# A two-layer hybrid decoder trunk: two mLSTM operands turned on TensorE instead of VectorE, and the loads and orders of the first two chunks rearranged

## The chip, the cores and the metric

The kernel runs on one core of one Trainium2 chip. The metric is the device time of one launch in microseconds (us), from the first to the last instruction of the program. Below, PE is TensorE's matmuls, PEld its weight loads, DVE is VectorE, ACT is ScalarE, POOL is GpSimd and SP is the sync engine, whose queue issues nearly all transfers.

## The reference

Two layers run over 256 tokens of 1024 features, all in float32. Each layer is a half-weighted SwiGLU, a mixer of three parallel branches, another half-weighted SwiGLU and a gated embedding:

```python
for l in range(DEPTH):
    x = x + 0.5 * swiglu(rms_norm(x, norm_ffn1[l]), ffn1_w_gu[l], ffn1_w_down[l])
    x = x + hybrid_mixer(rms_norm(x, norm_mix[l]), w_in[l], ...)
    x = x + 0.5 * swiglu(rms_norm(x, norm_ffn2[l]), ffn2_w_gu[l], ffn2_w_down[l])
    gate = jax.nn.sigmoid(rms_norm(x, norm_ple[l]) @ ple_w_gate[l])
    x = x + gate * (p[l] @ ple_w_proj[l])
return rms_norm(x, final_norm)
```

The mixer multiplies the normed tokens by one wide matrix `w_in` and splits the columns: a short gated convolution, an mLSTM with four heads (queries and keys of 128, values of 256), an indexed sparse attention that keeps the 64 best keys of each query, and three sigmoid gates that merge the branches.

## The kernel before

**Weights.** Each float32 weight tile that a transfer brings (`raw`, five buffers) is split in two: `wh` is a copy in the matmul type that ScalarE makes (L157), `wl` is the remainder that VectorE makes (L158). Each has four buffers of 4 x 512 columns. Every product is then three matmuls, L203, L204 and L205 in `mm3` (or six at L391 in the down projection). A `raw` buffer is free for the next transfer only when VectorE has made its `wl`.

**Stages.** In a feed-forward, `gate_up(c)` makes chunk c of 256 hidden columns for both token blocks, and `down_mm` adds the chunk before it into four accumulators. The first chunk of the first layer has loads of its own: four `raw` tiles (`first_gu`), split in eight pieces (`first_split`), with the tokens' transposes between them. In the mixer, `project` runs one block of 512 columns of `w_in` at a time: 4608, 5120, then the mLSTM queries (1536) and keys (2048), its values (2560, 3072), then 512, 1024, 0, 3584 and on.

**Side work.** What isn't a projection (the sparse attention `dsa`, the mLSTM gates and heads, the turns) are generators in two queues. `tick()` takes one step of the head of each queue, and `project` calls it four times, once for each half of the weights and each token block. A step's instructions are so traced between the matmuls of a projection. The order on each engine is then laid out by the tile planner, from this order as priority and from when it believes each operand to be ready; it may put a later instruction in front of an earlier one that it thinks is not ready. Every engine runs its own list strictly in order.

**The turn of queries and keys.** A projection leaves tokens on the partitions; the heads need features there. `qk_T` (L627) copies through `turn` (L277): 16 VectorE transposes at L281, each of 32 partitions, in four steps. `turn` is also used for the attention queries, the convolution and the feed-forwards. Elsewhere four TensorE transposes into one PSUM tile `tp` (two buffers) are followed by a copy on ScalarE, as at L551 and L553.

**The start.** ScalarE's queue loads the first 256 columns of x; SP loads the weights of chunk 0 and the rest of x. After them `load_gains` (L132) issues seven small transfers of gains and biases on SP, and turns the gains with one TensorE transpose (L117) and a copy. Only then do the loads of chunk 1 follow on SP. The final instruction of `first_split` on ScalarE is kept in `last`; `tc.issue_after(i)` puts all that is traced inside it, on the engine of `i`, behind `i`.

Of the kernel before, what the change touches and what calls it, by code (L numbers as in the profile page):

```python
# [10 lines left out]
F32 = mybir.dt.float32  # L11
F32R = mybir.dt.float32r
AF = mybir.ActivationFunctionType
# [3 lines left out]
P = 128  # L17
T = 256
NB = 2
# [18 lines left out]
def trunk_kernel(  # L38
# [7 lines left out]
    nc = tc.nc  # L46

    cpool = ctx.enter_context(tc.tile_pool(name="cpool", bufs=1))
# [9 lines left out]
    def nm(s):  # L58
        uid[0] += 1
        return f"{s}_{uid[0]}"  # L60
# [4 lines left out]
    def tps(shape=(P, 4, P)):  # L65
        return psum.tile(list(shape), F32, name=nm("tp"), tag="tp", bufs=2)
# [21 lines left out]
    x = []  # L88
# [3 lines left out]

    def load_x(q, c0, c1):
        for b in range(NB):
            last = q.dma_start(x[b][:, c0:c1], x_in[0, b * P:(b + 1) * P, c0:c1]).ins
        return last

    load_x(nc.scalar, 0, 256)

# [2 lines left out]
    mhalf = cpool.tile([P, 8], F32, name="mhalf")  # L102
    mh0 = cpool.tile([P, 8], F32, name="mh0")
    nc.vector.memset(mh0, -0.5)
    nc.scalar.activation(mhalf, mh0, AF.Copy)
    first_rows = cpool.tile([16, P], F32, name="first_rows")
    nc.sync.dma_start(first_rows, norm_ffn1.rearrange("l (k p) -> (l k) p", p=P))
    ident = cpool.tile([P, P], F32, name="ident")
    make_identity(nc, ident)
    gain_rows = cpool.tile([88, P], F32, name="gain_rows")  # L110
# [3 lines left out]
    def turn_gains(rows, c0):  # L114
        n = rows.shape[0]
        gps = tps((P, n))
        nc.tensor.transpose(gps, rows, ident[:n, :n])  # L117
        return nc.vector.tensor_copy(gains[:, c0:c0 + n], gps).ins
# [13 lines left out]
    def load_gains():  # L132
        r0 = 0
        for src in (norm_mix, norm_ffn2, norm_ple, mlstm_norm):
            nc.sync.dma_start(gain_rows[r0:r0 + 16, :], src.rearrange("l (k p) -> (l k) p", p=P))
            r0 += 16
        nc.sync.dma_start(gain_rows[r0:r0 + 24, :], conv_w.rearrange("l j (k p) -> (l j k) p", p=P))
        nc.sync.dma_start(bif[:, 0, :], mlstm_b_i.rearrange("l h -> h l"))
        nc.sync.dma_start(bif[:, 1, :], mlstm_b_f.rearrange("l h -> h l"))
        turn_gains(gain_rows, 16)  # L140

    zrow = cpool.tile([HM, T], F32, name="zrow")
    nc.vector.memset(zrow, 0.0)
# [8 lines left out]
    def split_tiles(shape):  # L152
        return (wpool.tile([P] + shape, F32R, name=nm("wh"), tag="wh"),
                wpool.tile([P] + shape, F32R, name=nm("wl"), tag="wl"))
# [23 lines left out]
    def gu_tiles(hi, lo):  # L178
        return [(hi[:, j].rearrange("p g n -> p (g n)"), lo[:, j].rearrange("p g n -> p (g n)"))
                for j in range(4)]  # L180

    def load_gu(src, k0, c):
# [4 lines left out]
            split(hi[:, :, g, :], lo[:, :, g, :], raws[g])  # L187
        return gu_tiles(hi, lo)

    def load_rows(src, k0):  # L190

        hi, lo = split_tiles([2, D])
        for k in range(2):
            raw = raw_tile([D])
            nc.sync.dma_start(raw, src[(k0 + k) * P:(k0 + k + 1) * P, :])
            split(hi[:, k, :], lo[:, k, :], raw)
        return [(hi[:, k, :], lo[:, k, :]) for k in range(2)]

# [78 lines left out]
    def turn(dst, src):  # L277

        for i in range(4):
            for j in range(4):  # L280
                nc.vector.transpose(  # L281
                    dst[32 * j:32 * j + 32].rearrange("p f (b i t) -> p b f i t", b=NB, i=4)[:, :, :, i, :],
                    src[32 * i:32 * i + 32].rearrange("p b (f j a) -> p b f j a", j=4, a=32)[:, :, :, j, :])
            if i < 3:
                yield

    def rms_scale(b, tag="r"):

# [30 lines left out]
    def ffn(xs, w_gu, w_down, next_norm, before_last=None, first=None):  # L319
        dn = None  # L320
        act = act_of(xs)

        def gate_up(c):
            at = mid([P, 2, 2, T], F32R)
            ps = [acc() for _ in range(NB)]
            groups = [(0, 4), (4, 4)]
            ks = {}

            def run(b, k0, n):
                for k in range(k0, k0 + n):  # L330
                    mm3(ps[b], act(b, k), ks[k], k == 0, k == KD - 1)

            s = half([P, NB, FCH])

            def finish(b):
                r = xs[b][2]
                nc.scalar.activation(s[:, b, :], ps[b][:, :FCH], AF.Silu, scale=r)  # L337
                nc.vector.scalar_tensor_tensor(s[:, b, :], ps[b][:, FCH:], r, s[:, b, :], op0=ALU.mult, op1=ALU.mult)  # L338

            def turn_pe(b):  # L340
                split_T(lambda f: s[:, b, f * P:(f + 1) * P], 2,
                        lambda f, m: at[:, 0, f:f + m, b * P:(b + 1) * P],
                        lambda f, m: at[:, 1, f:f + m, b * P:(b + 1) * P])
                return
                yield

            def turn_dve():
                st = half([P, 2, T])
                yield from turn(st, s)
                split(at[:, 0], at[:, 1], st)  # L350

            if c == 0 and first:
                ks.update(enumerate(first))
            else:
                for k0, n in groups:
                    for i, t in enumerate(load_gu(w_gu, k0, c)):
                        ks[k0 + i] = t
            if c == 0 and first:
                for k0 in range(0, KD, 2):
                    for b in range(NB):  # L360
                        run(b, k0, 2)
                for b in range(NB):
                    finish(b)
                turns = [turn_dve()]
            elif c == 0:
                for b in range(NB):
                    run(b, 0, KD)
                    tick()
                    finish(b)
                turns = [turn_dve()]  # L370
            else:
                for k0, n in groups:
                    for b in range(NB):
                        run(b, k0, n)
                        tick()
                for b in range(NB):
                    finish(b)
                turns = [turn_pe(b) for b in range(NB)] if c == NFC - 1 else [turn_dve()]
            queues[0].extend(turns)
            return at, turns  # L380

        def down_mm(act, ks, c, b):
            at, turns = act
            for t in turns:
                drain(t)
            for f in range(2):
                ah, al = (at[:, i, f, b * P:(b + 1) * P] for i in range(2))
                wh, wl = ks[f]
                for a, w in ((ah, wh), (ah, wl), (al, wh)):
                    for n in range(2):  # L390
                        nc.tensor.matmul(dn[b][n], a, w[:, n * 512:(n + 1) * 512],  # L391
                                         start=c == 0 and f == 0 and a is ah and w is wh,
                                         stop=c == NFC - 1 and f == 1 and a is al)
            tick()

        ats = {0: gate_up(0)}
        for c in range(NFC - 2):
            ats[c + 1] = gate_up(c + 1)
            if c == 0:
                dn = [[acc() for _ in range(2)] for _ in range(NB)]  # L400
            ks = load_rows(w_down, 2 * c)
            for b in range(NB):
                down_mm(ats[c], ks, c, b)
            del ats[c]
        c = NFC - 2
        ats[c + 1] = gate_up(c + 1)
        extra = before_last() if before_last else None
        k2 = [load_rows(w_down, 2 * (c + i)) for i in range(2)]
        new = []
        for b in range(NB):  # L410
            for i in range(2):
                down_mm(ats[c + i], k2[i], c + i, b)
            for n in range(2):
                xs_ = x[b][:, n * 512:(n + 1) * 512]
                nc.vector.scalar_tensor_tensor(xs_, dn[b][n], 0.5, xs_, op0=ALU.mult, op1=ALU.add)
            new.append(next_norm(b))
        return new, extra


    def mixer(l, xs, next_norm):  # L420
# [23 lines left out]
        for b in range(NB):  # L444
            q = ps1[b]
# [181 lines left out]
        def qk_T(nat):  # L627
            tt = mid([P, HM, T])
            qk.append(tt)
            yield from turn(tt, nat)  # L630
            yield

        for c0 in (1536, 2048):
            ps = proj(c0)
            nat = mid([P, NB, 512])
# [275 lines left out]
    first, ws = [], []  # L911
# [11 lines left out]
    for i in range(4):  # L923
        fetched.append(first_gu(2 * i))
        if i < 2:
            loaded = load_x(nc.sync, 256 * (i + 1), 512 * (i + 1))
    ts = [norm_tiles(b) for b in range(NB)]
    for i in range(4):
        his = [norm_part(b, G_FFN1, ts[b], 2 * i, 2)[-1] for b in range(NB)]
# [3 lines left out]
        with tc.issue_after(his[0]), tc.issue_after(gains_ready):  # L933
            last = first_split(fetched[i], 2 * (i % 2))
    with tc.issue_after(last):
        xs = [ts[b] + (rms_scale(b),) for b in range(NB)]
    with tc.issue_after(loaded):
        load_gains()
    for l in range(DEPTH):
        xs, _ = ffn(xs, ffn1_w_gu[l], ffn1_w_down[l], lambda b: norm_block(b, G_MIX + 8 * l),  # L940
                    first=first if l == 0 else None)
# [38 lines left out]
```

## Time and profile before

| | us |
|---|---|
| three runs | 1395.53, 1397.54 (median), 1398.69 |
| the profiled execution, its own time | 1398.2 |
| its span in the trace | 1396.2 |
| PE busy | 1363.6 (98%) |
| DVE busy | 1123.7 (80%) |
| ACT busy | 720.3 (52%) |

The span begins with the first recorded instruction and ends with the last; 2.0 us of the profiled time lie outside it. Matmuls overlap in the array, so their durations are longer than their spacing: back to back, a matmul of 512 columns starts every 0.23 us though it lasts 0.39 us. A busy PE in the page therefore only says that it had work; what a stall costs is read from the starts of its matmuls. In a timeline row the bracket gives the engine's idle time before the instruction and what ended it.

### The profile page before, as it was taken

The page shows a single profiled execution, that of the slowest core. Times are in us where ns is not written, and L with a number is a line of the kernel's source. Part 1 is how long each engine was busy: PE and PEld are TensorE (multiplying, and loading weights), DVE is VectorE, ACT ScalarE, POOL GpSimd, SP SyncE. Part 2 cuts the span into 40 slices and gives each one's busy share as a digit, 9 for nine tenths or more (in the row PEclk, how much of TensorE's full clock was granted, in tenths as well). Part 3 has the DMA queues.
Part 4 walks back from the last instruction along what each step waited for, and adds up shares of the span by engine and source line. Part 5 has one row for each costly group of instructions (what it writes and reads, how often), then busy time and mean ns, then how long its engine had stood idle before and what let it go on. Part 6 is the DMA issues. An engine that isn't in the chain of part 4 may idle for free.

```text
span 1396.2 us, 17264 instructions
## 1 busy us (share of the span) xinstructions
PE 1363.6 (98%) x6124; PEld 1111.8 (80%) x6124; DVE 1123.7 (80%) x2099; ACT 720.3 (52%) x1127; POOL 22.7 (2%) x42
## 2 busy tenths in 40 slices
PE   7999999799999999999999999998999999999997
PEld 6888888687788888888888888886768888888886
DVE  5978879979965688878788888799799556888876
ACT  6544465465454464444664444563655446444454
POOL 0000000000000000000000000000000000000000
PEclk9999999999999999999999999999999999999999
DMA  7766556254475546666555666554445655555661
GB/s 226 222 213 198 182 175 196 83 190 121 151 241 181 181 154 201 204 194 217 172 163 183 197 205 201 174 166 144 143 126 179 222 181 181 182 181 185 196 215 46
DMA packets 163427, 250.33 MB, mean 179 GB/s; under 512 B 7964, under 2 KB 101260, under 8 KB 163340
## 3 DMA queue, kind: packets, MB, share of 16 engines
q1 hardware_dynamic: 162700, 247.91, 55.3%
q8 instruction: 48, 0.79, 0.2%
q0 software_dynamic: 352, 1.06, 0.2%
q14 instruction: 39, 0.32, 0.1%
q10 hardware_dynamic: 288, 0.26, 0.1%
HBM read 248.14 MB, written 1.06 MB: 178 GB/s over the span
## 4 chain that ended last, share of the span: by engine, by line
PE 87%; DVE 10%; issue 1%; ACT 1%; DMA 0%; POOL 0%; SPq 0%; POOLq 0%; ACTq 0%; DVEq 0%
PE acc L205 22%; PE acc L204 22%; PE acc L203 22%; PE acc L391 17%; DVE mid L281 4%; DVE wl L158 2%; PE tp L262 2%; DVE score L504 1%; DVE m L503 1%; PE acc L675 1%; PE acc L458 1%; DMA x<-in_x_dram 0%; ACT wh L157 0%; DVE mid L722 0%; DVE big L524 0%
## 5 line engine op out<-in xcount | busy, mean ns | idle before, releaser
L158 DVE TENSOR_TENSOR wl<-raw,wh 128x1024 fp32r<-128x1024 f32 (+1 forms) x472 | 555.0, 1210 | 105.2 <-ACT wh L157 103.0
L157 ACT ACTIVATE wh<-raw 128x1024 fp32r<-128x1024 f32 (+1 forms) x472 | 473.9, 1043 | 227.4 <-issue 92.6
L204 PE MATMUL acc<-wl,xh 128*128 128x512 f32 (+1 forms) x1384 | 541.9, 392 | 13.8 <-DVE wl L158 13.8
L203 PE MATMUL acc<-wh,xh 128*128 128x512 f32 (+1 forms) x1384 | 546.4, 395 | 0.9 <-ACT wh L157 0.9
L205 PE MATMUL acc<-wh,xl 128*128 128x512 f32 (+1 forms) x1384 | 541.7, 392 | 0.0
L204 PEld LDWEIGHTS acc<-wl,xh 128*128 128x128 f32 x1384 | 262.3, 190 | 67.9 <-DVE wl L158 15.9
L203 PEld LDWEIGHTS acc<-wh,xh 128*128 128x128 f32 x1384 | 262.2, 189 | 58.1 <-issue 3.9
L205 PEld LDWEIGHTS acc<-wh,xl 128*128 128x128 f32 x1384 | 262.4, 190 | 53.8
L281 DVE STREAM_TRANSPOSE half<-half 32x128 f32<-32x128 f32 x640 | 193.6, 303 | 9.5
L391 PE MATMUL acc<-wh,mid 128*128 128x512 f32 x704 | 198.3, 391 | 0.0
L391 PEld LDWEIGHTS acc<-wh,mid 128*128 128x128 f32 x704 | 131.0, 188 | 27.4 <-ACT mid L265 0.9
L391 PE MATMUL acc<-wl,mid 128*128 128x512 f32 x352 | 108.6, 390 | 0.0
L338 DVE SCALAR_TENSOR_TENSOR half<-acc,r,half 128x256 f32<-128x256 f32 x88 | 42.1, 481 | 78.8 <-ACT half L337 78.8
L157 ACT ACTIVATE mid<-half 128x512 fp32r<-128x512 f32 x40 | 25.3, 633 | 142.9 <-DVE half L281 142.9
L337 ACT ACTIVATE half<-acc,r 128x256 f32<-128x256 f32 x88 | 41.7, 473 | 107.9 <-PE acc L205 107.8
L391 PEld LDWEIGHTS acc<-wl,mid 128*128 128x128 f32 x352 | 66.1, 188 | 13.9
L281 DVE STREAM_TRANSPOSE mid<-mid 32x256 f32<-32x256 f32 x160 | 69.7, 436 | 3.4
L272 ACT ACTIVATE xh<-tp,gains 128x128 fp32r<-128x128 f32 x128 | 41.7, 362 | 19.7 <-PE tp L262 11.3
L204 PE MATMUL acc<-wl,big 128*128 128x512 f32 x128 | 50.0, 390 | 0.0
L205 PE MATMUL acc<-wh,big 128*128 128x512 f32 x128 | 49.8, 389 | 0.0
L203 PE MATMUL acc<-wh,big 128*128 128x512 f32 x128 | 49.8, 389 | 0.0
L273 DVE SCALAR_TENSOR_TENSOR xl<-tp,gains,xh 128x128 fp32r<-128x128 f32 x128 | 40.7, 346 | 8.8 <-ACT xh L272 8.0
(180 smaller groups left out, 722.8 us busy)
## 6 DMA issues: line engine op xcount, KB each, us to landing
raw<-in_ffn_w_gu_dram SPq DMA_DIRECT2D x172, 512.0 KB, 5.1
raw<-in_w_in_dram SPq DMA_DIRECT2D x128, 512.0 KB, 4.3
raw<-in_ffn_w_down_dram SPq DMA_DIRECT2D x88, 512.0 KB, 4.6
raw<-in_mlstm_w_out_dram SPq DMA_DIRECT2D x16, 512.0 KB, 4.2
raw<-in_w_o_dram SPq DMA_DIRECT2D x16, 512.0 KB, 4.1
raw<-in_ple_w_gate_dram SPq DMA_DIRECT2D x16, 512.0 KB, 5.2
raw<-in_attn_w_out_dram SPq DMA_DIRECT2D x8, 512.0 KB, 3.6
raw<-in_conv_w_out_dram SPq DMA_DIRECT2D x8, 512.0 KB, 4.7
```

What stands on the lines that cost most here:

```text
L157: made = nc.scalar.activation(hi, v, AF.Copy).ins
L158: nc.vector.tensor_tensor(lo, v, hi.bitcast(F32), op=ALU.subtract)
L203: nc.tensor.matmul(ps, ah, wh, start=start, stop=False)
L204: nc.tensor.matmul(ps, ah, wl, start=False, stop=False)
L205: nc.tensor.matmul(ps, al, wh, start=False, stop=stop)
L262: turned[0] = nc.tensor.transpose(tp[:, j, :], src_of(k0 + j), ident).ins
L272: his.append(nc.scalar.activation(hi, tp[:, j:j + 1, :], AF.Copy, scale=g).ins)
L273: nc.vector.scalar_tensor_tensor(lo, tp[:, j:j + 1, :], g, hi.bitcast(F32), op0=ALU.mult, op1=ALU.subtract)
L281: nc.vector.transpose(dst[32 * j:32 * j + 32].rearrange("p f (b i t) -> p b f i t", b=NB, i=4)[:, :, :, i, :], src[32 * i:32 * i + 32].rea ...
L337: nc.scalar.activation(s[:, b, :], ps[b][:, :FCH], AF.Silu, scale=r)
L338: nc.vector.scalar_tensor_tensor(s[:, b, :], ps[b][:, FCH:], r, s[:, b, :], op0=ALU.mult, op1=ALU.mult)
L391: nc.tensor.matmul(dn[b][n], a, w[:, n * 512:(n + 1) * 512], start=c == 0 and f == 0 and a is ah and w is wh, stop=c == NFC - 1 and f == 1 ...
```

## The change

The queries' and keys' turn becomes four TensorE transposes and one ScalarE copy for each token block, in two steps instead of four. A first, unused Silu is put on ScalarE at the very start. The seven transfers of `load_gains` move behind the weight loads of the second down projection, and the transpose of the gains moves to chunk 5. ScalarE's instructions of chunk 1 are put behind the last split of chunk 0.

```diff
@@ at the start
+    junk0 = cpool.tile([P, 8], F32, name="junk0")
+    nc.scalar.activation(junk0, mh0, AF.Silu)
     nc.scalar.activation(mhalf, mh0, AF.Copy)
@@ def load_gains():
-        turn_gains(gain_rows, 16)
@@ def load_rows(src, k0):
-            nc.sync.dma_start(raw, src[(k0 + k) * P:(k0 + k + 1) * P, :])
+            fetched_last[0] = nc.sync.dma_start(raw, src[(k0 + k) * P:(k0 + k + 1) * P, :]).ins
@@ new
+    def pe_turn(dst, src):
+
+        for b in range(NB):
+            tp = tps()
+            for f in range(4):
+                nc.tensor.transpose(tp[:, f, :], src[:, b, f * P:(f + 1) * P], ident)
+            nc.scalar.activation(dst[:, :, b * P:(b + 1) * P], tp, AF.Copy)
+            yield
@@ def ffn
         for c in range(NFC - 2):
-            ats[c + 1] = gate_up(c + 1)
+            with ExitStack() as order:
+                if first and c == 0:
+                    order.enter_context(tc.issue_after(last))
+                ats[c + 1] = gate_up(c + 1)
+            if first and c == 5:
+                turn_gains(gain_rows, 16)
...
             ks = load_rows(w_down, 2 * c)
+            if first and c == 1:
+                with tc.issue_after(fetched_last[0]):
+                    load_gains()
@@ def qk_T(nat):
-            yield from turn(tt, nat)
-            yield
+            yield from pe_turn(tt, nat)
@@ before the layers
-    with tc.issue_after(loaded):
-        load_gains()
```

## Rows read from the trace of the kernel before

**Rows 1.** The page: busy time of each engine, and the chain's shares by engine.

```profile
PE 1363.6 (98%) x6124; PEld 1111.8 (80%) x6124; DVE 1123.7 (80%) x2099; ACT 720.3 (52%) x1127; POOL 22.7 (2%) x42
...
PE 87%; DVE 10%; issue 1%; ACT 1%; DMA 0%; POOL 0%; SPq 0%; POOLq 0%; ACTq 0%; DVEq 0%
```

**Rows 2.** Table by stretch of 5 us in the first layer's mixer, columns first.

```profile
core 0: us, PE busy (x) PEld busy (x) DVE busy (x) ACT busy (x) POOL busy (x), PEclk, DMA share, GB/s
270.00:275.00 5.00, 1.03 (x5) 0.53 (x3) 4.71 (x12) 1.63 (x2) 0.00 (x0) 0.94 0.02 8
275.00:280.00 5.00, 4.72 (x11) 3.76 (x12) 5.00 (x12) 2.94 (x7) 0.00 (x0) 0.50 0.65 197
...
340.00:345.00 5.00, 3.81 (x12) 2.96 (x13) 4.94 (x12) 3.92 (x6) 0.00 (x0) 0.76 0.17 27
```

**Rows 3.** The chain in order of time: start, us, what; one run of matmuls.

```profile
38.85 5.44 PE acc L391 x24
```

**Rows 4.** Timeline of PE, both mixers: start us, us, engine line op, tiles, shape, count.

```profile
261.85 0.39 PE L203 MATMUL acc<-wh,xh 128*128 128x512 f32 x1
265.28 0.50 PE L204 MATMUL acc<-wl,xh 128*128 128x512 f32 x1 [3.04 <-DVE wl L158]
...
275.28 0.80 PE L204 MATMUL acc<-wl,xh 128*128 128x512 f32 x1 [4.25 <-DVE wl L158]
...
280.14 1.05 PE L658 MATMUL acc<-mid,mid 128*128 128x256 f32 x2
...
949.28 0.39 PE L203 MATMUL acc<-wh,xh 128*128 128x512 f32 x1
...
967.16 0.66 PE L658 MATMUL acc<-mid,mid 128*128 128x256 f32 x2
```

**Rows 5.** Timeline of DVE in the first layer's mixer.

```profile
242.31 0.87 DVE L281 STREAM_TRANSPOSE mid<-mid 32x256 f32<-32x256 f32 x2
...
263.53 0.44 DVE L281 STREAM_TRANSPOSE mid<-mid 32x256 f32<-32x256 f32 x1
263.99 2.36 DVE L158 TENSOR_TENSOR wl<-raw,wh 128x1024 fp32r<-128x1024 f32 x2
...
308.34 0.75 DVE L710 SCALAR_TENSOR_TENSOR mid<-acc,r,mid 128x512 f32<-128x512 f32 x1 [3.23 <-PE acc L205]
```

**Rows 6.** Groups of instructions: count, busy us, mean ns of one, idle before, releaser.

```profile
L281 DVE STREAM_TRANSPOSE mid<-mid 32x256 f32<-32x256 f32 x160 | 69.7, 436 | 3.4
L553 ACT ACTIVATE half<-tp 128x512 f32<-128x512 f32 x12 | 7.0, 584 | 2.4 <-PE tp L551 2.4
```

**Rows 7.** Timeline of PE around four transposes of the sparse attention.

```profile
308.14 0.60 PE L551 MATMUL tp<-ident,big 128*128 128x128 f32 x4
...
308.81 0.40 PE L204 MATMUL acc<-wl,xh 128*128 128x512 f32 x1
```

**Rows 8.** Timeline of ACT, a weight copy that waits for its transfer.

```profile
268.78 1.06 ACT L157 ACTIVATE wh<-raw 128x1024 fp32r<-128x1024 f32 x1 [10.53 <-DMA raw<-in_w_in_dram]
```

**Rows 9.** Timeline of PE at the start.

```profile
16.51 0.39 PE L204 MATMUL acc<-wl,xh 128*128 128x512 f32 x1
20.45 0.27 PE L117 MATMUL tp<-ident,gain_rows 88*128 88x88 f32 x1 [3.55 <-issue]
...
28.13 0.50 PE L204 MATMUL acc<-wl,xh 128*128 128x512 f32 x1 [0.53 <-DVE wl L158]
```

**Rows 10.** Timeline of SP's queue at the start (issues of transfers).

```profile
8.56 0.60 SPq L135 DMA_DIRECT2D gain_rows<-in_norm_mix_dram  x1
...
13.76 2.05 SPq L173 DMA_DIRECT2D raw<-in_ffn_w_gu_dram  x4
...
41.42 9.21 SPq L173 DMA_DIRECT2D raw<-in_ffn_w_gu_dram  x4
```

**Rows 11.** Timeline of ACT at the start.

```profile
17.77 1.06 ACT L157 ACTIVATE wh<-raw 128x1024 fp32r<-128x1024 f32 x1 [3.71 <-DMA raw<-in_ffn_w_gu_dram]
18.74 0.61 ACT L272 ACTIVATE xh<-tp,gains 128x128 fp32r<-128x128 f32 x2
...
24.11 1.28 ACT L337 ACT_TABLE_LOAD   x1 [1.03 <-PE acc L205]
...
25.78 1.05 ACT L157 ACTIVATE wh<-raw 128x1024 fp32r<-128x1024 f32 x1
```

More of the change, by code (lines that the diff above doesn't have):

```diff
@@ L94, in load_x @@
         for b in range(NB):
-            last = q.dma_start(x[b][:, c0:c1], x_in[0, b * P:(b + 1) * P, c0:c1]).ins
-        return last
+            q.dma_start(x[b][:, c0:c1], x_in[0, b * P:(b + 1) * P, c0:c1])
     load_x(nc.scalar, 0, 256)
@@ L188, in load_gu @@
         return gu_tiles(hi, lo)
+    fetched_last = [None]
     def load_rows(src, k0):
@@ L925, in trunk_kernel @@
         if i < 2:
-            loaded = load_x(nc.sync, 256 * (i + 1), 512 * (i + 1))
+            load_x(nc.sync, 256 * (i + 1), 512 * (i + 1))
     ts = [norm_tiles(b) for b in range(NB)]
```

## The prediction

> **What bounds the kernel now.** I read the page's busy shares first, then its chain, then the table by stretch, and only then the timelines of the stretches that the table picked out. PE is busy 98% of the span and carries 87% of the chain [rows 1]; the reader should see that a change pays only where PE stalls, and costs wherever it adds to PE. DVE carries 10% of the chain, so some stretch hangs on it. The table shows where: between 270 and 275 us PE has 1.03 us of work while DVE is full (4.71), and in the next 5 us PE runs at a granted clock of 0.50, which is the lower of its two levels, 1.2 GHz [rows 2]. PE's timeline names the wait: it stands for 3.04 and 4.25 us, both times for `wl` of L158 [rows 4]. DVE's timeline shows why `wl` is late. From 242.31 to 263.53 it does 24 of the 32 turns of queries and keys, alternating with the top-k of the sparse attention, and only then the next two splits [rows 5]. The wait for raw weights on ACT, 10.53 us [rows 8], follows from it: a raw buffer comes free when DVE has split it. The second layer repeats this from 949.28 on [rows 4].
>
> The price of these stalls: back to back, 24 matmuls take 5.44 us [rows 3], 0.227 each. From 261.85 to 280.14 the trace starts 36 matmuls of 512 columns, worth 8.2 us; they take 18.3, so 10.1 us are lost, the stand-stills and the slow clock behind them. In the second layer, from 949.28 to 967.16, there are also 36: 17.9 less 8.2 is 9.7 [rows 3, 4]. Together 19.8 us.
>
> **The turn moved, what it removes.** A turn is 16 instructions of 436 ns [rows 6], two a layer: 32 x 0.436 = 14.0 us less on DVE in each layer. Take the same order with the turns cut out. The splits of 263.99 have 24 turns in front of them, 10.5 us, and so would start at 253.5; PE first misses them at 265.28 - 3.04 = 262.2 [rows 4, 5], so they are ready (two take 2.36) about 6 us ahead. The next splits have all 32 turns in front, and move up by 14.0 against a second stall that needs 4.25 plus what the first gave back, 7.3 in all. The raw buffers come free earlier by the same 10 to 14 us, so the transfers behind the wait on ACT do too. Both stalls go, and the slow clock with them. The order after the change isn't known, since the planner lays it out anew. If it is worse, the bound is that half of the 19.8 stays (as if only the first pair of splits moved up); it can't give more than 19.8 here. I take 19.8, because the margin is some 6 us and the turns are pure ballast in this queue.
>
> What is late next? DVE has a second full stretch in each layer, where PE waits for the softmax: between 340 and 345 it loses 1.19 us idle and, at a clock of 0.76, 0.24 x 3.81 = 0.9 more [rows 2], 2.1 us, and the like in the second layer. At 308.34 DVE had caught up and waited 3.23 us for PE [rows 5]; work saved before that point isn't carried over it. I leave this loss where it is: 0, with 4.2 as the gain if a new order heals it.
>
> **What it adds.** Each turn is two groups of four transposes, so eight groups over both layers. The group at 308.14 is followed by one matmul of 512 columns before the row at 308.81: 0.67 - 0.227 = 0.44 us on PE [rows 3, 7]. 8 x 0.44 = 3.5 us, in full on the path, as PE is the bound. ACT gets eight copies like L553, 584 ns each [rows 6], 4.7 us beside an engine that is 52% busy [rows 1]: nothing, while the weight copies run ahead. If they don't, each copy stands 0.58 in front of a split: at most 4.7. The copy waits for PE, and behind it on ACT wait the copies of weights for later matmuls; PE in turn would wait for a `tp` buffer at a third group if the first was not yet copied. From both sides: 0, if ACT is as free as its share says, and 10.5 us a layer, the longest wait of a weight copy [rows 8], if a turned group's copy is queued behind one. I take 0: with the turns off DVE that wait itself moves up and shrinks.
>
> On PE's price the trace is short: four transposes show 0.60 us from first start to last end [rows 7]. The Trainium skill (TensorE: Matmul & The Clock Gate, Part 4: PE-mode transpose) gives about 275 ns for one in a kernel's context; 32 of them unoverlapped would be an estimated 8.8 us instead of 3.5 and the sum 1382. The trace disagrees: they start closer together than that.
>
> **The start.** From 16.51 to 28.13 PE starts 19 matmuls of 512 columns, worth 4.3 us, in 11.6: 7.3 us are lost [rows 3, 9]. Three things hold it. PE stands 3.55 us in front of L117, whose rows come by the seven small transfers [rows 9]; that transpose moves to chunk 5, where the rows have long landed, and costs the same there. SP issues the seven from 8.56 on and the weights of chunk 1 only at 13.76 [rows 10]; these now go 5.2 us sooner. And ACT waits 3.71 us, to 17.77, for the first of these weights, with the last pieces of chunk 0 behind it in its list [rows 11]; the new order puts chunk 1 behind them. So the work that began at 18.74 can begin at about 14.6, when PE's last transposes are done (an estimate: ACT's idle time begins at 17.77 - 3.71 = 14.06): 4.1 us sooner. The table load of 1.28 us at 24.11 goes, because the Silu at the start fetches that table in idle time. The 1.03 us in front of it go too, as PE is early; but one weight copy, 1.06, which was done at 17.77, now comes after. 4.1 + 1.28 + 1.03 - 1.06 = 5.4 us. Ends: 3.3, if two more copies of 1.05 go in front of the one PE needs, and 7.3, all of the loss. I take 5.4.
>
> On the table load, the row shows 1.28 us and the next instruction right behind it [rows 11]. The Trainium skill (ScalarE: Activation LUTs, What ACT_TABLE_LOAD costs) counts 2.66 us with a drain; by that the sum would be 1.4 us lower. No drain shows here.
>
> The seven transfers now stand on SP between the weights of the second down projection and those of chunk 3, issued at 41.42. They took 5.2 us of SP's queue. There, four issues take 9.21 us, where four without waits took 2.05 [rows 10]: SP spends 7.2 us waiting for raw buffers, and that covers them. Price 0; if the cover is gone, 5.2 once.
>
> **Sum.** 1398.2 (profiled time) - 19.8 - 5.4 + 3.5 = 1376.5. The median of the runs is 0.7 under the profiled time; I say 1376. About 0.2%, 2.8 us, is what a measurement of this kernel can tell from no change.
>
> **The rivals.**
> - *Half of it.* The planner's new order leaves one of the two stalls in each layer: 9.9 less gain, 1386. For it: the top-k stays in front of the splits. Against: the margin of 6 us. 0.10.
> - *More.* The second full stretch heals as well (4.2) and the start gives 7.3: 1370. For it: DVE has slack; against: it waits for PE at 308.34 [rows 5]. 0.06.
> - *The gain is given back later.* PE comes some 8 us earlier to the softmax in each layer while DVE is not earlier there: 16 us back, 1392. Against: DVE loses 14 us of work, more than PE's path. 0.05.
> - *Slower.* PE's transposes wait for ScalarE. `tp` has two buffers and ACT's list is in order; a copy behind a weight copy that waits 10.53 us [rows 8] stops PE, and each restart costs slow clock, as the 2.4 us lost at 0.50 in 275 to 280 [rows 2]. Two layers: 2 x 12.9 = 26, 1402. It decides from 21.7 us in all (19.8 + 5.4 - 3.5), 10.9 a layer. For it: such a wait exists; against: it comes after 258, when the values' first projection, where the turns now sit, is over. 0.06.
> - *The clock falls around the transposes.* If a group dropped the clock, it would be low for the 9 us of the four groups and 5 more in each layer, as in 275 to 280 [rows 2]: half of 14 twice, 14 us, 1390. After the group at 308.14 the next matmuls last 0.40, those of full clock, 2.4 GHz [rows 7]. The Trainium skill (TensorE: Matmul & The Clock Gate, Part 4) says that transposes don't count as busy for the clock gate; here no row shows a fall behind one. 0.03.
>
> **How the numbers follow.** Forecast 0.70, at 1376, by its bounds 1370 to 1383. The range goes to 1369 and 1391; the slower case and the far part of the given-back one are left out. Faster by over 0.2%: 0.70 + 0.10 + 0.06 + 0.03 and 0.02 of the given-back case, 0.91; within: 0.03; slower: 0.06.
>
> **What would show it.** After the change: no `wl` wait over 1 us on PE in the mixer, granted clock 1.00 through it; 96 turns of the form on `mid` left of 160 (64 fewer over both layers), and 32 new transposes of 0.11 us spacing; ACT's new copies at 0.58 us; no L117 at the start, one Silu table load less, and PE's first steady matmul of chunk 1 near 22.7. Wrong would be: waits of PE for ACT at a `tp`, a stall that grows at the softmax, or a hole in the feed-forward near 45 us, behind the seven transfers.

## The result and the profile after

| | before | after |
|---|---|---|
| median of the runs, us | 1397.57 (1395.53 to 1398.69) | 1374.26 (1374.13 to 1376.19) |
| the profiled execution, its own time | 1398.2 | 1374.13 |
| its span | 1396.2 | 1372.3 |
| mean granted clock | 0.991 | 0.998 |

The changed kernel takes 0.9835 of the time before (95% interval 0.9819 to 0.9851), 23.3 us less. The forecast was 1376.0, from 1369 to 1391.

The code has grown, so lines have moved: the three matmuls of `mm3` are L205 to L207 (L203 to L205 before), the 32x32 turn is L283 (L281), the head's first matmul L676 (L658), the down projection L402 (L391), the softmax's transposes L570 (L551). The new transposes are L294 and their copies L295.

First the page of the changed kernel: busy time by engine, the chain's shares, and two groups (count, busy us and mean ns, idle before, releaser).

```profile
PE 1357.8 (99%) x6156; PEld 1110.4 (81%) x6156; DVE 1095.6 (80%) x2035; ACT 722.6 (53%) x1135; POOL 24.9 (2%) x42
...
PE 93%; DVE 5%; ACT 1%; issue 1%; POOL 0%; POOLq 0%; ACTq 0%
...
L206 PE MATMUL acc<-wl,xh 128*128 128x512 f32 (+1 forms) x1384 | 538.3, 389 | 0.7 <-DVE wl L158 0.7
...
L283 DVE STREAM_TRANSPOSE mid<-mid 32x256 f32<-32x256 f32 x96 | 41.8, 436 | 1.5
```

PE's share of the chain rose from 87% to 93%, DVE's fell from 10% to 5% [rows 1]. Of the 160 turns of this form [rows 6] 96 are left. PE has 32 instructions more and 5.8 us less busy time, since fewer of its matmuls ran at the lower clock (mean granted clock 0.991 before, 0.998 now). The remainders `wl` kept PE waiting 13.8 us in all, by the page of before; now it is 0.7, at the start:

```profile
L204 PE MATMUL acc<-wl,xh 128*128 128x512 f32 (+1 forms) x1384 | 541.9, 392 | 13.8 <-DVE wl L158 13.8
```

The table by stretch of 5 us, changed kernel, through the stretch that answers to [rows 2] and through the softmax behind it:

```profile
core 0: us, PE busy (x) PEld busy (x) DVE busy (x) ACT busy (x) POOL busy (x), PEclk, DMA share, GB/s
255.00:260.00 5.00, 5.00 (x23) 4.14 (x23) 4.76 (x13) 2.39 (x3) 1.16 (x1) 1.00 0.25 91
260.00:265.00 5.00, 5.00 (x23) 4.13 (x22) 3.10 (x3) 2.31 (x4) 0.00 (x0) 1.00 0.81 243
...
325.00:330.00 5.00, 3.08 (x11) 2.33 (x12) 4.89 (x13) 4.63 (x6) 0.00 (x0) 0.84 0.23 52
330.00:335.00 5.00, 5.00 (x21) 3.77 (x19) 4.84 (x11) 2.49 (x3) 0.00 (x0) 0.81 0.65 206
```

DVE is as full as before until 260 us, then it has air (3.10 of 5), and PE works through at the full clock. The stall at the softmax is still there, 14 us earlier.

VectorE's list has a new order as well. Before, no split stands between 242.31 and 263.99 [rows 5]; now two come at 242.69 and 246.05, among the rounds of the top-k. The first of them:

```profile
242.69 1.22 DVE L158 TENSOR_TENSOR wl<-raw,wh 128x1024 fp32r<-128x1024 f32 x1
```

PE's timeline of the changed kernel, both mixers. L503 is a matmul group of the indexed attention just ahead of the turns, L676 the first matmul of the mLSTM heads; of the four groups of new transposes in each layer the first is shown:

```profile
238.36 1.14 PE L503 MATMUL acc<-akT,half 64*128 64x256 f32 x8
...
242.67 0.60 PE L294 MATMUL tp<-ident,mid 128*128 128x128 f32 x4
...
266.38 0.59 PE L676 MATMUL acc<-mid,mid 128*128 128x256 f32 x2
...
917.08 1.14 PE L503 MATMUL acc<-akT,half 64*128 64x256 f32 x8
...
945.11 0.59 PE L676 MATMUL acc<-mid,mid 128*128 128x256 f32 x2
```

The same attention group in the kernel before (L484 there):

```profile
243.97 1.14 PE L484 MATMUL acc<-akT,half 64*128 64x256 f32 x8
...
931.40 1.14 PE L484 MATMUL acc<-akT,half 64*128 64x256 f32 x8
```

From that attention group to the heads PE needs 266.38 - 238.36 = 28.0 us. Before, the way from 243.97 to 280.14 [rows 4] took 36.2. In the second layer it was 967.16 - 931.40 = 35.8 and is 28.0.

The start of the changed kernel, by SP's queue, ACT and PE:

```profile
8.57 6.00 SPq L173 DMA_DIRECT2D raw<-in_ffn_w_gu_dram  x4
...
35.06 0.42 SPq L136 DMA_DIRECT2D gain_rows<-in_norm_mix_dram  x1
```

```profile
14.20 0.64 ACT L274 ACTIVATE xh<-tp,gains 128x128 fp32r<-128x128 f32 x2 [0.57 <-PE tp L264]
...
18.49 1.05 ACT L157 ACTIVATE wh<-raw 128x1024 fp32r<-128x1024 f32 x1
19.44 0.46 ACT L348 ACTIVATE half<-acc,r 128x256 f32<-128x256 f32 x1
```

```profile
19.70 0.39 PE L207 MATMUL acc<-wh,xl 128*128 128x512 f32 x1
20.90 0.73 PE L205 MATMUL acc<-wh,xh 128*128 128x512 f32 x2 [0.81 <-ACT wh L157]
22.38 0.50 PE L206 MATMUL acc<-wl,xh 128*128 128x512 f32 x1 [0.75 <-DVE wl L158]
```

The weights of chunk 1 are issued from 8.57 on, not from 13.76 [rows 10]. ACT finds them landed at 18.49 and goes on to its Silu without a table load [rows 11]. The matmul that stood at 28.13 [rows 9] starts at 22.38, 5.75 us earlier. The first matmul of the down projection goes from 38.69 to 32.95, 5.7 us earlier; below this is "the first down projection".

### The profile page after: what moved, and what is told of

The parts are those of the page before. It is cut to its first block, busy times and chain, and to the rows that moved or that the text cites. A ratio compares the mean times of both kernels' runs of the same rounds, so it can differ in the third digit from the quotient of the medians.

```text
span 1372.3 us, 17274 instructions
## 1 busy us (share of the span) xinstructions
PE 1357.8 (99%) x6156; PEld 1110.4 (81%) x6156; DVE 1095.6 (80%) x2035; ACT 722.6 (53%) x1135; POOL 24.9 (2%) x42
## 3 DMA queue, kind: packets, MB, share of 16 engines
q0 software_dynamic: 352, 1.06, 0.2%
HBM read 248.14 MB, written 1.06 MB: 182 GB/s over the span
## 4 chain that ended last, share of the span: by engine, by line
PE 93%; DVE 5%; ACT 1%; issue 1%; POOL 0%; POOLq 0%; ACTq 0%
PE acc L205 24%; PE acc L207 24%; PE acc L206 24%; PE acc L402 18%; PE tp L264 2%; DVE mid L283 2%; DVE wl L158 1%; PE acc L693 1%; PE acc L477 1%; DVE mid L740 0%; DVE big L543 0%; DVE mx L551 0%; PE acc L128 0%; PE tp L570 0%; DVE big L558 0%
## 5 line engine op out<-in xcount | busy, mean ns | idle before, releaser
L205 PE MATMUL acc<-wh,xh 128*128 128x512 f32 (+1 forms) x1384 | 544.8, 394 | 0.8 <-ACT wh L157 0.8
L207 PE MATMUL acc<-wh,xl 128*128 128x512 f32 (+1 forms) x1384 | 538.5, 389 | 0.0
L205 PEld LDWEIGHTS acc<-wh,xh 128*128 128x128 f32 x1384 | 260.6, 188 | 57.3 <-issue 3.9
L207 PEld LDWEIGHTS acc<-wh,xl 128*128 128x128 f32 x1384 | 260.3, 188 | 53.0
L283 DVE STREAM_TRANSPOSE half<-half 32x128 f32<-32x128 f32 x640 | 193.9, 303 | 9.5
L402 PE MATMUL acc<-wh,mid 128*128 128x512 f32 x704 | 198.5, 392 | 0.0
L402 PEld LDWEIGHTS acc<-wh,mid 128*128 128x128 f32 x704 | 131.0, 188 | 27.3 <-ACT mid L267 0.9
L402 PE MATMUL acc<-wl,mid 128*128 128x512 f32 x352 | 108.6, 390 | 0.0
L402 PEld LDWEIGHTS acc<-wl,mid 128*128 128x128 f32 x352 | 66.1, 188 | 13.8
L274 ACT ACTIVATE xh<-tp,gains 128x128 fp32r<-128x128 f32 x128 | 41.7, 363 | 19.8 <-PE tp L264 11.4
L207 PE MATMUL acc<-wh,big 128*128 128x512 f32 x128 | 49.9, 390 | 0.0
L205 PE MATMUL acc<-wh,big 128*128 128x512 f32 x128 | 49.8, 389 | 0.0
L283 DVE STREAM_TRANSPOSE mid<-mid 32x256 f32<-32x256 f32 x96 | 41.8, 436 | 1.5
```

What stands on the lines that cost most here:

```text
L205: nc.tensor.matmul(ps, ah, wh, start=start, stop=False)
L207: nc.tensor.matmul(ps, al, wh, start=False, stop=stop)
L274: his.append(nc.scalar.activation(hi, tp[:, j:j + 1, :], AF.Copy, scale=g).ins)
L283: nc.vector.transpose(dst[32 * j:32 * j + 32].rearrange("p f (b i t) -> p b f i t", b=NB, i=4)[:, :, :, i, :], src[32 * i:32 * i + 32].rea ...
L402: nc.tensor.matmul(dn[b][n], a, w[:, n * 512:(n + 1) * 512], start=c == 0 and f == 0 and a is ah and w is wh, stop=c == NFC - 1 and f == 1 ...
```

## The experiments

All edits are to the changed kernel unless said otherwise. The runs were made on three chips; the kernel before took 1397.8, 1397.6 and 1397.5 us beside them. Where no interval is given, one execution was taken.

### One half of the change alone

e1 puts the queries and keys back on VectorE and keeps the start.

```diff
-            yield from pe_turn(tt, nat)
+            yield from turn(tt, nat)
+            yield
```

> The changed kernel, but with the queries' and keys' turn back on VectorE (the start's changes alone). Theory (the turn's load on VectorE stalls PE; the parts add up): 5.7 us under the kernel before, 1391.8 us, with the two stalls of some 3 and 4 us per mixer back in front of a split weight, and PE's first steady matmul of chunk 1 at 22.4. Rival (the start's gain is waited for again in the mixer, because VectorE bounds it there): within 1.5 us of the kernel before, 1397, with longer stalls in the first mixer. Rival (the planner's new layout after the start made the mixer's gain): near the changed kernel, 1376, and no stalls.

Measured: 1391.22, ratio 0.9956 (0.9943 to 0.9968). Its table by stretch:

```profile
255.00:260.00 5.00, 1.97 (x10) 1.31 (x9) 4.74 (x12) 0.00 (x0) 0.00 (x0) 1.00 0.00 0
...
265.00:270.00 5.00, 0.73 (x4) 0.31 (x2) 4.74 (x12) 1.63 (x2) 0.00 (x0) 0.83 0.01 4
270.00:275.00 5.00, 5.00 (x12) 3.98 (x13) 5.00 (x11) 3.09 (x7) 0.00 (x0) 0.50 0.76 211
```

Both stand-stills are back (PE 1.97 and 0.73 of 5, DVE full), and the slow clock with them. So they belong to the turns on VectorE and not to the start. The turn is worth 1391.22 - 1374.26 = 17.0 us, and the start alone 1397.8 - 1391.2 = 6.6.

e2 is the kernel before with nothing but the queries and keys on TensorE.

```diff
@@ def qk_T (kernel before)
-            yield from turn(tt, nat)
-            yield
+            yield from pe_turn(tt, nat)
```

> The kernel before with the queries' and keys' turn on TensorE and ScalarE, nothing else. Theory: the changed kernel's time plus the start's 5.7 us, 1380.0 us; no stall of PE for a split weight between 240 and 285 us, granted clock 1.00 there, and the start as in the kernel before (the matmul of 28.13 stays). Rival (part of the mixer's gain needs the earlier start): over 1384.

Measured: 1380.98, ratio 0.9879 (0.9866 to 0.9893). PE is full in every stretch from 240 to 285 us. The turn alone takes off 1397.8 - 1381.0 = 16.8 us, and 16.8 + 6.6 is the whole change's 23.3 within 0.1: the parts add. The start is worth 1380.98 - 1374.26 = 6.7 here, a little more than the 5.7 by the first down projection; the profiled execution of this kernel reached it at 40.1 us against 38.7 before.

### How much margin there is on VectorE

e3 turns only the queries on TensorE and leaves the keys on VectorE.

```diff
-            yield from pe_turn(tt, nat)
+            if len(qk) == 1:
+                yield from pe_turn(tt, nat)
+            else:
+                yield from turn(tt, nat)
+                yield
```

> The changed kernel with the queries turned on TensorE and the keys still on VectorE: 16 of 32 VectorE turns stay in each mixer. Theory (the turns are load in front of the split weights, and there was margin): the first pair of splits moves up by 7.0 us where PE missed them by 3.0, the second by 7.0 where it needs 7.3, so under 1 us of stall a mixer is left, and PE has 4 groups of transposes less, 1.8 us: 1372.5 to 1374.5, the same as the changed kernel or a little faster. Rival (the gain goes with the work taken off VectorE): half of 18 us is gone, 1383.

Measured: 1372.84, ratio 0.9821 (0.9807 to 0.9834). Its table:

```profile
260.00:265.00 5.00, 5.00 (x24) 4.14 (x23) 5.00 (x12) 2.78 (x7) 0.00 (x0) 1.00 0.68 197
...
270.00:275.00 5.00, 4.32 (x25) 3.23 (x25) 4.93 (x9) 2.94 (x4) 1.15 (x1) 1.00 0.87 288
```

With 7 us of turns back, DVE is full once more, but PE loses only 0.68 us, once, inside the mLSTM heads (it waits for their `wt`, L689) and not for a split weight. Half of the move is enough: a margin like the 6 us of the prediction's step is there, and the second half buys nothing that can be measured.

One rival is left open. The turns went and the planner laid out VectorE's list anew, with splits among the rounds of the top-k, and no run takes the turns out in the old order. By the prediction's arithmetic the load alone would do; how much the new order adds isn't shown.

### ScalarE's and TensorE's price

e12 makes each of the eight copies three times over.

```diff
-            nc.scalar.activation(dst[:, :, b * P:(b + 1) * P], tp, AF.Copy)
+            for _ in range(3):
+                nc.scalar.activation(dst[:, :, b * P:(b + 1) * P], tp, AF.Copy)
```

> The changed kernel with each of ScalarE's eight copies of a turned group made three times over (16 more of 0.39 to 0.58 us, 3 us more of ScalarE a layer). Theory (ScalarE has slack there, but the fourth group of transposes gets its buffer only some 2 us before TensorE would wait): TensorE waits at most 1 us for a turned buffer in each layer; 1374 to 1376.5. Rival (ScalarE's list is on the path): each added copy pushes the copies of weights behind it, 1379 to 1384.

Measured: 1375.27, ratio 0.9841 (0.9827 to 0.9854), not told apart from the change. PE is full through 235 to 280 us and waits for no turned buffer. The copies' price of 0 holds, with three times as many.

e10 makes each of the 32 transposes five times over.

```diff
-            for f in range(4):
+            for f in 5 * (0, 1, 2, 3):
```

> The changed kernel with each of the 32 new transposes on TensorE made five times over (128 more). Theory (TensorE is the bound and a transpose costs it 0.109 us there): 1374.3 + 128 x 0.109 = 1388.3, with the granted clock at 1.00 through 240 to 280 us. Rival by the page's 275 ns for each (an estimate): 1409. Rival (the clock falls around long runs of transposes): a granted clock of 0.50 behind a group and over 1395. Rival (the transposes fit in slack): under 1380.

Measured: 1388.15, ratio 0.9937 (0.9923 to 0.9951). PE's timeline and the table of the stretch:

```profile
242.41 2.35 PE L294 MATMUL tp<-ident,mid 128*128 128x128 f32 x20
```

```profile
240.00:245.00 5.00, 5.00 (x34) 4.41 (x33) 4.79 (x18) 3.51 (x6) 0.00 (x0) 1.00 0.40 136
245.00:250.00 5.00, 5.00 (x33) 4.41 (x33) 4.96 (x19) 2.03 (x6) 1.71 (x2) 1.00 0.61 193
```

The 128 added transposes cost 1388.15 - 1374.26 = 13.9 us, 0.109 each, in full on the path; four make the 0.44 us of the prediction. The Trainium skill (TensorE: Matmul & The Clock Gate, Part 4: PE-mode transpose) gives about 275 ns for one. That is the duration that a record has here too (272 ns median), but the next one starts 0.109 us later, and that is the price. Even twenty in a row leave the granted clock at 1.00, 2.4 GHz: the rival of a falling clock is out for groups of this length.

### The start taken apart

Each of the next four undoes one piece of the start.

e5 takes the early Silu out.

```diff
-    nc.scalar.activation(junk0, mh0, AF.Silu)
```

> The changed kernel without the early Silu. Read at the first matmul of the first down projection, which stands at 32.9 to 33.6 us in the four kernels with the changed start and at 38.7 in the kernel before. Theory (the table load is on the path there): 1.28 us later, 34.2 to 34.9, with a table load in front of the first Silu near 19.4. Rival (ScalarE has slack there): 33 to 33.6.

Measured: 1377.12; first down projection at 35.9. ACT, PE and the table by 2 us:

```profile
19.67 1.28 ACT L347 ACT_TABLE_LOAD   x1
```

```profile
22.43 0.73 PE L204 MATMUL acc<-wh,xh 128*128 128x512 f32 x2 [2.22 <-ACT wh L156]
```

```profile
24.00:26.00 2.00, 2.00 (x7) 1.60 (x6) 2.00 (x3) 2.00 (x3) 0.00 (x0) 0.63 0.56 176
26.00:28.00 2.00, 2.00 (x6) 1.54 (x6) 1.93 (x7) 0.99 (x2) 0.00 (x0) 0.52 0.82 262
```

The load delays what stands behind it on ACT, and PE's wait grows from 0.81 to 2.22. The matmul of 22.38 stands at 23.69, 1.3 us later, as was expected. More came on top: PE then ran mostly at 1.2 GHz for some 4 us (0.63 and 0.52), which cost 1.6, and the first down projection is 2.9 later. Whether the longer wait brought the clock down isn't shown: e11, with the changed kernel's own waits, lost the same 1.6 us there (last section).

e6 takes out the order that puts chunk 1's instructions on ScalarE behind chunk 0's.

```diff
-                if first and c == 0:
-                    order.enter_context(tc.issue_after(last))
```

> The changed kernel without putting ScalarE's work of chunk 1 behind the last split of chunk 0. Theory (ScalarE's list would again hold a wait for chunk 1's weights in front of chunk 0's last pieces): some 2 to 4 us later at the first down projection, 35 to 37, with a stall of PE near 17. Rival (with the weights issued at 8.6 the wait is over in time, and the order is worth nothing): 33 to 33.6.

Measured: 1376.51; first down projection at 33.8, 0.9 later than with the change. ACT and PE:

```profile
15.23 1.06 ACT L157 ACTIVATE wh<-raw 128x1024 fp32r<-128x1024 f32 x1 [1.50 <-DMA raw<-in_ffn_w_gu_dram]
```

```profile
18.72 0.50 PE L206 MATMUL acc<-wl,xh 128*128 128x512 f32 x1 [0.85 <-DVE wl L158]
```

The copy for chunk 1 is back in front of the last ones of chunk 0, as in [rows 11], but it waits 1.50 us and not 3.71, because the weights come earlier. The theory's figure was too high.

e7 lets SP issue the seven small transfers ahead of chunk 1's weights again.

```diff
+    with tc.issue_after(loaded):
+        load_gains()
@@ in the feed-forward
-            if first and c == 1:
-                with tc.issue_after(fetched_last[0]):
-                    load_gains()
```

Here and in e8 and e9 `loaded` is again the last load of x on SP, as in the kernel before.

> The changed kernel, but the seven small transfers are issued early again, in front of the weights of chunk 1; the transpose of the gains stays in chunk 5. Theory (the transfers cost SP 5.2 us, but ScalarE takes chunk 1's weights only from 18.5 on, and they landed at 17.8 in the kernel before): under 1 us later, 33 to 34.2 at the first down projection. Rival (the 5.2 us of SP's queue were on the path): 37 to 38.

Measured: 1374.77; first down projection at 33.5. SP's weights go out at 13.93 again, and PE's two waits (0.72 and 0.75) are those of the changed kernel. The planner put the gains' transpose at 20.45 in this kernel, ahead of chunk 5, and PE didn't wait for it. So the 5.2 us on SP are, by themselves, not on the path.

e8 adds to e7 the early transpose of the gains, before the first feed-forward.

```diff
+    with tc.issue_after(loaded):
+        load_gains()
+        turn_gains(gain_rows, 16)
@@ in the feed-forward
-            if first and c == 5:
-                turn_gains(gain_rows, 16)
```

> As the kernel with early transfers, and the transpose of the gains is early again too. Theory (PE's wait at that transpose is the main loss of the start): PE stands some 3.5 us near 17, runs on the slow clock after it, and reaches the first down projection 3.5 to 5 us later, 36.5 to 38.5. Rival (the wait is hidden behind ScalarE's and VectorE's work for chunk 1): 33 to 34.5.

Measured: 1374.44; first down projection at 33.1. I had expected the wait of [rows 9] back, and it did not come: the transpose ran at 15.54 without any wait.

```profile
15.54 0.24 PE L119 MATMUL tp<-ident,gain_rows 88*128 88x88 f32 x1
```

It was not what PE stood for. The trace of before agrees. It gives a landing for four of the five transfers of the gain rows, the last at 14.6 us (issued at 10.91, 3.65 later), 5.9 before L117. That transpose writes one of the two `tp` buffers, and it starts just behind the first of these two reads of `tp`, which stand behind ScalarE's instruction of 18.74 [rows 11]:

```profile
20.01 0.60 DVE L273 SCALAR_TENSOR_TENSOR xl<-tp,gains,xh 128x128 fp32r<-128x128 f32 x2
```

That left a combination. In e6 the copy stood in front, but its weights came early; in e7 the weights came late, but the copy stood behind. e9 does both, keeps the Silu, and holds the gains' transpose late.

```diff
+    with tc.issue_after(loaded):
+        load_gains()
@@ in the feed-forward
-                if first and c == 0:
-                    order.enter_context(tc.issue_after(last))
...
             if first and c == 5:
-                turn_gains(gain_rows, 16)
+                with tc.issue_after(fetched_last[0]):
+                    turn_gains(gain_rows, 16)
...
-            if first and c == 1:
-                with tc.issue_after(fetched_last[0]):
-                    load_gains()
```

> The changed kernel with three parts of the start undone or altered: the seven small transfers go out ahead of chunk 1's weights as before, chunk 1's copies on ScalarE are no longer ordered behind the last of chunk 0, and the gains' transpose stays behind the loads of a later chunk. The Silu at the start stays. Theory (TensorE's wait at the start was ScalarE's: its list held a copy that waited for chunk 1's weights ahead of the last copies of chunk 0, and the seven transfers made these weights late; either half alone is harmless, the gains' transpose only stood in the same place): ScalarE waits 3 to 4 us for raw weights and TensorE stands 3 to 4 us between 16 and 21 us with no gains' transpose near; first down-projection matmul at 36.0 to 38.5 us (32.9 with the change) and 1377 to 1380. Rival (the gains' transpose was the wait): with that transpose late TensorE stands less than 1 us there; first down-projection matmul at 33 to 34 us, 1374 to 1376.

Measured: 1381.18; first down projection at 38.4. SP, ACT and PE:

```profile
14.27 2.05 SPq L174 DMA_DIRECT2D raw<-in_ffn_w_gu_dram  x4
```

```profile
18.38 1.06 ACT L158 ACTIVATE wh<-raw 128x1024 fp32r<-128x1024 f32 x1 [4.15 <-DMA raw<-in_ffn_w_gu_dram]
19.34 0.61 ACT L275 ACTIVATE xh<-tp,gains 128x128 fp32r<-128x128 f32 x2
19.84 1.15 ACT L158 ACTIVATE wh<-raw 128x512 fp32r<-128x512 f32 x2
```

```profile
17.60 0.39 PE L208 MATMUL acc<-wh,xl 128*128 128x512 f32 x1
20.52 0.50 PE L206 MATMUL acc<-wh,xh 128*128 128x512 f32 x1 [2.53 <-ACT wh L158]
```

Here it is again without the gains' transpose: ACT waits 4.15 us for chunk 1's weights, and behind that wait lie the last pieces of chunk 0 (19.34, 19.84), for which PE stands until 20.52. The gains' transpose ran at 26.08, without a wait. PE's 2.53 us are less than the 3 to 4 that were expected, and the time is 1.2 us above the expected range. Either half alone cost 0.5 to 0.9 us at the first down projection, no more than its scatter: e1, e3, e4, e10 and e12, with the change's own start, reached it between 32.7 and 33.6, and e11 only at 35.2, of which a fallen clock cost 1.6. Both together cost 5.4, and the clock fell here too (PE started a matmul every 0.43 us from 22.78 to 25.77), which is some 1.6 of it. The wait put down to "issue" at L117 in [rows 9] was ScalarE's list.

### The stretch that the change left: the softmax

e4 moves the convolution's first turn, which VectorE makes ahead of the softmax, to TensorE as well.

```diff
-            yield from turn(uT, ccn)
-            yield
+            yield from pe_turn(uT, ccn)
```

> The changed kernel with the convolution's first turn (16 VectorE transposes, 7 us in one block) on TensorE too, in the same way. Theory (VectorE's load in front of the softmax makes PE's second stall in each mixer): both second stalls go, some 3.5 us in the first layer and 2 in the second, against 4 more groups of transposes at 0.44: 1370.5 us. Rival (the softmax's place is set by the order of steps, not by that load): the stalls stay and PE pays 1.8: 1376.

Measured: 1372.43, ratio 0.9818 (0.9805 to 0.9831). Table and PE's timeline:

```profile
325.00:330.00 5.00, 5.00 (x28) 4.16 (x27) 4.88 (x12) 2.46 (x4) 0.00 (x0) 1.00 0.01 3
...
340.00:345.00 5.00, 4.56 (x16) 2.18 (x15) 4.93 (x9) 3.41 (x6) 0.00 (x0) 1.00 0.50 145
```

```profile
342.73 1.07 PE L477 MATMUL acc<-half,avn 128*64 128x512 f32 x2 [0.44 <-ACT half L572]
```

The stall at the softmax is gone; 0.44 us of a new wait stands behind it. From the second pair of score matmuls to the second group of value matmuls PE takes 23.00 us in each layer, against 26.73 and 25.15 with the change. Of these 5.9 us the four more groups of transposes take 1.8; the median is 1.8 lower, less than the 3.8 that were expected. The rest went to small losses, 0.7 us of them at the start of the profiled execution.

e11 joins e3 and e4: queries and the convolution's first turn on TensorE, keys on VectorE.

> The changed kernel with the keys turned on VectorE again (queries on TensorE) and the convolution's first turn on TensorE: as many transposes on TensorE as in the change, put where VectorE is late at the softmax. Theory (one turn taken off VectorE before each of the two late stretches is enough): the keys give back 1.5, the convolution's turn takes 1.8: 1371 (1370 to 1372.5), no wait of TensorE over 1 us at the softmax and in the stretch 255 to 285 us. Rival (the two need the same slack on VectorE, since the keys' 7 us come ahead of the convolution): waits for wl of 1 to 4 us come back in the stretch 260 to 285 us and it is 1374 to 1378.

Measured: 1371.01 (1369.69 to 1373.08), ratio 0.9808 (0.9795 to 0.9822). PE has no wait over 1 us from 235 to 345 us, as was expected. It is the fastest, with as many transposes as the change, 3.3 us below it. That is 0.24%, about what can be told from nothing; e3, e4 and e11 can't be told from each other.

## Why the prediction was right, step by step

- **The mixer stalls, 19.8 forecast.** Right. The way from the attention group to the heads shrank by 8.2 us in the first layer and 7.7 in the second. With the transposes' 1.8 a layer added back, the stalls were 9.9 and 9.5, against 10.1 and 9.7. e1 brings them back, e3 shows the margin. The step counted with the old order of VectorE's list and the planner gave another, so that the load alone does it is argued and not shown.
- **The transposes, 3.5.** Right, by e10 to the hundredth of a microsecond for each.
- **ScalarE's copies, 0.** Right. ACT takes the second group's copy at 249.74, 3 us after that group; e12 shows room for more.
- **The start, 5.4.** The size was right, 5.75 at the matmul of 28.13. The 4.1 us that were read from ScalarE's list came out as 4.5: the work of 18.74 began at 14.20. The reading of the causes was not right. I named three, the gains' transpose, SP's seven transfers and the order on ScalarE, as if each had a part. The transpose has none (e8, e9), and the other two cost something only together (e6, e7, e9).
- **The table load, 1.28 in that sum.** It fits: with the 1.03 in front of it and the weight copy of 1.06 it makes 1.25, and 5.75 - 4.5 is 1.2; e5 shows 1.3 at its matmul. The 2.9 of e5 at the first down projection hold 1.6 of slow clock, which one execution can't put down to the load.
- **SP's transfers at their new place, 0.** Right: PE stands for nothing between 24 and 52 us.
- **The softmax, 0, with 4.2 as the most.** Right in the first layer (26.7 us both times). The sign "granted clock 1.00 through it" failed there: it was 0.84 and 0.81 behind the stall that was left in. In the second layer the stall kept its length, 1.9 us, but the clock behind it did not fall, and the stretch took 1.5 us less (25.15 against 26.69). That is the luck of this execution, as the last section tells.

The forecast parts are -5.4, -16.3 and 0; the measured ones -5.7, -15.9 and -1.5, with 0.6 more behind the stalls, where before the clock was still slow. That makes 23.7, against 23.9 by the spans. The rivals: "half" fell with the stalls, "given back" with the unchanged softmax, "slower" with PE's timeline, which shows no wait for a `tp`, and with e12, "the clock falls" with e10. "More" did not come: the softmax stall is as long as it was.

## What to carry to other kernels

Cost a move between engines by the stretch in which the crowded engine ends last, and move only until that wait is gone: half of this move did (e3), and with the other half spent in the next such stretch e11 came out 3.3 us lower, at the edge of what can be told. In lists that run strictly in order, a wait shows up in front of an innocent instruction, so ask what stands ahead of the operand's maker on its own engine. Undo suspected causes singly and in pairs, since two that are each harmless can make the whole wait together.

## What the runs showed that I had not expected

The price of a short stall differs from one occurrence to the next. PE's timeline of the changed kernel shows the softmax stall in both layers, and the table the clock behind it in the second:

```profile
326.72 0.33 PE L570 MATMUL tp<-ident,big 128*128 128x128 f32 x1 [1.90 <-DVE big L558]
...
1005.45 0.33 PE L570 MATMUL tp<-ident,big 128*128 128x128 f32 x1 [1.91 <-DVE big L558]
```

```profile
1005.00:1010.00 5.00, 4.36 (x21) 3.51 (x22) 4.97 (x11) 4.21 (x6) 0.00 (x0) 1.00 0.26 84
```

Two stalls of the same length stand behind the same work. After the first the granted clock fell (0.84 and 0.81 in the table above), after the second it stayed at 1.00, and the stretch was 1.6 us shorter. In the other kernels that keep this stall the stretch took either some 25.1 us or some 26.7, in either layer. e11 shows the same at the start: the two waits of the changed kernel, 0.81 and 0.75, and behind them a clock of 0.62 for 4 us where the change had 1.00; its first down projection came at 35.2.

```profile
21.58 0.73 PE L205 MATMUL acc<-wh,xh 128*128 128x512 f32 x2 [0.81 <-ACT wh L157]
23.06 0.50 PE L206 MATMUL acc<-wl,xh 128*128 128x512 f32 x1 [0.75 <-DVE wl L158]
```

```profile
24.00:28.00 4.00, 4.00 (x13) 3.12 (x12) 3.90 (x10) 1.79 (x2) 0.00 (x0) 0.62 0.87 263
```

Even one kernel in one execution does both. In e1 PE waits equally long in front of the same work in both layers; behind the first wait the clock stays at 1.00 (260 to 265 us), behind the second it falls (0.76 from 945 to 950 us).

```profile
259.86 0.50 PE L206 MATMUL acc<-wl,xh 128*128 128x512 f32 x1 [3.03 <-DVE wl L158]
...
946.97 0.50 PE L206 MATMUL acc<-wl,xh 128*128 128x512 f32 x1 [3.02 <-DVE wl L158]
```

What decides it the runs don't tell. It means that 1 to 2 us between two single executions of this kernel, e6's 2.3 us among them, are no evidence for an edit, and e3's 1.4 between medians is no larger: e3's profiled execution kept the clock in both layers, the change's in one.
